# Moving a root chain to the end of a stage and reordering the last tiles of a hybrid DeltaNet and attention kernel

## Chip, cores and metric

The kernel runs on one core of a Trainium2 chip. A core has TensorE (PE, matrix products into the PSUM memory), VectorE (DVE), ScalarE (ACT), GpSimd (POOL) and SyncE (SP, which here issues most DMA transfers). The metric is the device time of one execution in microseconds; the median of three executions counts. All times in the text are microseconds, and those with a place ("at 354.0") are counted from the first instruction of the profiled execution.

## What is computed

Two layers over 512 latent tokens and 256 context tokens, 1024 wide, all in float32. Layer 0 is a bidirectional gated DeltaNet, layer 1 is grouped-query attention with a rotary embedding; each ends in a gated residual addition, and a last RMS norm gives the output.

```python
u = rms_norm(h, norm_g) * (1 + scale) + shift               # both layers
# layer 0
p = u @ w_in                                                # q: 8 heads, k: 8, v: 16, z: 16, of 128
qkv = silu(centred_dwconv(p[..., :DN_CONV_DIM], conv_w))    # 5 taps along the tokens
q = q * rsqrt(sum(q * q, -1) + 1e-6)                        # query norms; k likewise
o = forward and backward gated delta rule, in chunks of 64 tokens, context first, then latents
y = (rms_norm(o, o_norm_g) * silu(z)) @ w_out
# layer 1
y = (softmax(q k^T / sqrt(128)) v * silu(z)) @ w_out        # 8 query heads, 2 key heads
h = h + gate * y
return rms_norm(h_lat, final_norm_g)                        # (1, 512, 1024)
```

## The kernel before

Products that need float32 accuracy are made of three passes: each operand is split into a high and a low part, and high by high, high by low and low by high are summed in PSUM (the names wh and wl are the two parts of a weight, uh and ul those of the activations).

**The stage of the heads** lies between about 185 and 574 us. After the eight key heads, forty heads of the DeltaNet layer are worked in the order `zqzqzqqzqqzqqzvvzvvzvvzvvzvvzvvzvvzvvzzz`. Each is 48 matmuls for the 512 latent tokens and the 256 context tokens (L758, two PSUM banks out of four, so that a head takes the banks of the head two places before). A z head then needs a tanh on ACT (L781) and a gate step on DVE (L790), which reads the bank for the last time and so frees it. A v head needs a copy of the middle tap on ACT (L765), four taps on DVE (L773), a tanh on ACT (L783) and a step on DVE (L792), which frees the bank. Before each head its weights are loaded by SP (L739) and split by ACT (L744) and by DVE or POOL (L747). Beside the heads run other jobs: POOL solves triangular systems column by column (L643, L644, for three pairs of token tiles), multiplies the decays with the products of queries and keys (L545, into buffers named df, of which there are four, then stored by SP, L727), ACT computes the decays (L570, L572) from rows that SP loads (L557), and SP moves the results.

The sums of squares of the query heads come from PE (L810), and ACT copies them into `rq` (128 partitions by 6 tiles by 8 heads, 48 columns). The inverse root of `rq` is taken by `rsqrt_steps` (L185 to L204), eleven DVE instructions in a row that each read what the one before wrote. The text calls these the chain. The first later readers of `rq` are L1355 and L1088.

The order of all this on each engine is written by a planner in the kernel. Every job is a `Piece` with an engine, a cost, a due time, the pieces it comes after, the buffers it takes or holds, and an earliest time `since`. `ready_at` gives the time at which a piece could start on the planner's own clock (DVE pieces get a margin of 0.5), and `written_out` always writes next the piece that can start first, and among equals the one due first. On the chip every engine then works its list strictly in that order. The chain is one such piece of DVE (L1044), with a cost of 2.4 and a due time of `N * SLOT`, that is 40 x 8.8 = 352, and with no earliest time other than the end of the last copy into `rq`.

**The recurrence** follows (from about 574 us): its opening is the products of L1184 on PE, copies on ACT and the vd products on DVE (L1194). Then come the output projection of layer 0 (L1325) and the second layer.

**The last stage** begins at about 1151 us, where the attention's last gate step is done. For each of four tiles of 128 tokens, PE sums the output projection (L1845) into two PSUM banks of 512 columns. Per half, `finish_half` multiplies it by the gate (DVE, L1987), adds it to the residual `hs` (DVE, L1988) and squares and sums it on ACT (L1989). `finish_norm` turns the two sums into an inverse root by eight small DVE instructions (L1996 to L2000). Tiles 0 to 2 are scaled by that root and by the norm's weights `fg` in one DVE instruction (L2015) and sent by SP (L2006). For tile 3 each half is weighed by `fg` early (L2026); after the root, ACT scales the first half (L2028) and DVE the second (L2030), and ACT's and SP's queues send them. DVE works tile by tile: all of a tile's steps, then the next tile's. The row `jko` of two buffers holds the products of tiles 0 to 3 in turn.

Of the kernel before, what the change touches and what calls it, by code (L numbers as in the profile page):

```python
# [8 lines left out]
F32 = mybir.dt.float32  # L9
# [8 lines left out]
P = 128  # L18
D = 1024
# [67 lines left out]
def backbone(tc, a, out):  # L87
# [945 lines left out]
    for t, due in enumerate((170, 200, 230, 260, 290, 320)):  # L1033
# [5 lines left out]
        for v in range(2):  # L1039
# [4 lines left out]
    Piece("DVE", 2.4, N * SLOT, lambda: [f_() for f_ in rsqrt_steps(rq.rearrange("p t h -> p (t h)"), 1.0)], after=[last["rq", h] for h in range(QH)])  # L1044
# [857 lines left out]
    for u in range(32 + 4):  # L1902
# [82 lines left out]
    def finish_half(t, nh, jk):  # L1985
        c = slice(nh * 512, nh * 512 + 512)
        V.tensor_tensor(jk[:, c], acc[t][nh], gate1[:, 0, c], ALU.mult)  # L1987
        V.tensor_tensor(hs[t][:, c], hs[t][:, c], jk[:, c], ALU.add)  # L1988
        S.activation(jk[:, c], hs[t][:, c], AF.Square, accum_out=ss[:, t, nh:nh + 1])  # L1989
        if nh == 0:  # L1990
            V.tensor_scalar(ss[:, t, 0:1], ss[:, t, 0:1], 1.0 / D, EPS, ALU.mult, ALU.add)  # L1991

    def finish_norm(t):

        x, y, w = (f2.tile([P, 1], F32, tag=f"fr{i}", name=f"fr{i}_{t}") for i in range(3))
        V.tensor_scalar(x, ss[:, t, 1:2], 1.0 / D, ss[:, t, 0:1], ALU.mult, ALU.add)  # L1996
# [11 lines left out]
    for t in range(4):  # L2008
        jk = f2.tile([P, D], F32, tag="jko", name=f"jko{t}")
        if t < 3:  # L2010
            for k in range((KT, 6, 0)[t], KT):
                out_block(k, t, acc[t])
            for nh in range(2):
                finish_half(t, nh, jk)
            V.scalar_tensor_tensor(jk, hs[t], finish_norm(t), fg, ALU.mult, ALU.mult)  # L2015
            send(t, jk, slice(0, D), dma)
            if t == 0:
                load_hs(3)
        else:
            halves_ = [slice(0, 512), slice(512, D)]  # L2020
            hg = wp.tile([P, D], F32, tag="w", name="hg", bufs=3)
            for nh in range(2):
                for k in range(KT):
                    out_block(k, t, acc[t], (nh,))
                finish_half(t, nh, jk)
                V.tensor_tensor(hg[:, halves_[nh]], hs[t][:, halves_[nh]], fg[:, halves_[nh]], ALU.mult)  # L2026
            r = finish_norm(t)
            S.activation(hg[:, halves_[0]], hg[:, halves_[0]], AF.Copy, scale=r)  # L2028
            send(t, hg, halves_[0], nc.scalar.dma_start)
            V.tensor_scalar(hg[:, halves_[1]], hg[:, halves_[1]], r, None, ALU.mult)  # L2030
            send(t, hg, halves_[1], dma)
    written.__exit__(None, None, None)
    f2_c.__exit__(None, None, None)
    at_c.__exit__(None, None, None)
# [31 lines left out]
```

## Time and profile before

| | us |
|---|---|
| median of three executions (1184.9, 1194.69, 1189.23) | 1189.23 |
| the profiled execution | 1189.06 |
| its span, first to last instruction | 1187.2 |
| PE busy in the span | 1131.2 |
| mean granted clock of TensorE over the span | 0.987 |

In the rows of the order of time the columns are start, duration (both in us), engine, line, operation, output <- inputs, shapes, count, and in brackets the engine's idle time before it with what ended that. PEld is the loading of weights into PE, and runs beside it. In the table of stages the columns are the stretch, its length, then busy us and instructions of PE, PEld, DVE, ACT and POOL, then the granted clock of TensorE (1.00 is full), the busy share of the DMA engines and GB/s. In the list of waits the three numbers are total us, times and the longest. In the rows of one tile they are count, then shortest, median and longest duration in ns, and the first and last start.

### The profile page before, as it was taken

The page shows a single profiled execution, that of the slowest core. Times are in us where ns is not written, and L with a number is a line of the kernel's source. Part 1 is how long each engine was busy: PE and PEld are TensorE (multiplying, and loading weights), DVE is VectorE, ACT ScalarE, POOL GpSimd, SP SyncE. Part 2 cuts the span into 40 slices and gives each one's busy share as a digit, 9 for nine tenths or more (in the row PEclk, how much of TensorE's full clock was granted, in tenths as well). Part 3 has the DMA queues.
Part 4 walks back from the last instruction along what each step waited for, and adds up shares of the span by engine and source line. Part 5 has one row for each costly group of instructions (what it writes and reads, how often), then busy time and mean ns, then how long its engine had stood idle before and what let it go on. Part 6 is the DMA issues. An engine that isn't in the chain of part 4 may idle for free. (4 is left out here: it accounts for less than half of the span.)

```text
span 1187.2 us, 27636 instructions
## 1 busy us (share of the span) xinstructions
PE 1131.2 (95%) x10739; PEld 919.0 (77%) x10739; DVE 801.9 (68%) x1723; ACT 721.1 (61%) x1885; POOL 584.0 (49%) x443
## 2 busy tenths in 40 slices
PE   3998999999979999999999999899999999999995
PEld 1676778888868888888666666688887889999884
DVE  2669565889898777763588888546557466667646
ACT  3343333889666873874478998785753246666721
POOL 0130004499998998441285586555744244130900
PEclk9899999999999999999999999999999999999998
DMA  9477976866549544979599996475744112101323
GB/s 332 153 240 240 298 218 187 238 165 167 147 138 284 182 133 131 292 218 286 157 257 248 248 274 162 158 224 185 241 155 134 36 54 72 36 19 54 107 71 89
DMA packets 171124, 208.72 MB, mean 176 GB/s; under 512 B 12497, under 2 KB 126322, under 8 KB 170226
## 3 DMA queue, kind: packets, MB, share of 16 engines
q1 hardware_dynamic: 150914, 195.19, 55.7%
q10 hardware_dynamic: 20080, 11.77, 3.3%
q8 instruction: 85, 1.39, 0.5%
q14 instruction: 45, 0.37, 0.1%
HBM read 166.16 MB, written 40.67 MB: 174 GB/s over the span
## 5 line engine op out<-in xcount | busy, mean ns | idle before, releaser
L1325 PE MATMUL po<-woh,y 128*128 128x512 f32 x384 | 129.3, 401 | 0.7 <-ACT y L1301 0.7
L1167 POOL TENSOR_TENSOR S<-S,glb 128x512 f32<-128x512 f32 x80 | 81.7, 1042 | 70.0 <-PE ks L1158 70.0
L1274 POOL TENSOR_TENSOR wol<-wo,woh 128x1024 fp32r<-128x1024 f32 x32 | 77.1, 2412 | 54.6 <-ACT woh L1267 51.6
L644 POOL TENSOR_TENSOR X<-X,tmp 128x62 f32<-128x62 f32 (+15 forms) x93 | 97.0, 1043 | 7.3
L773 DVE SCALAR_TENSOR_TENSOR acc_v<-g_v,cwv,acc_v 128x510 f32<-128x510 f32 (+3 forms) x128 | 78.2, 615 | 31.9 <-ACT acc_v L765 28.2
L758 PE MATMUL g_v<-uh,wh_v 128*128 128x512 f32 (+1 forms) x256 | 89.4, 349 | 6.6 <-DVE sil_z L790 6.6
L643 POOL TENSOR_TENSOR tmp<-L,X 128x62 f32<-128x62 f32 (+15 forms) x93 | 86.4, 929 | 6.8
L758 PE MATMUL g_z<-uh,wh_z 128*128 128x512 f32 (+1 forms) x256 | 88.7, 346 | 0.0
L758 PE MATMUL g_v<-ul,wh_v 128*128 128x512 f32 (+1 forms) x256 | 87.2, 341 | 0.0
L758 PE MATMUL g_v<-uh,wl_v 128*128 128x512 f32 (+1 forms) x256 | 87.0, 340 | 0.0
L758 PE MATMUL g_z<-ul,wh_z 128*128 128x512 f32 (+1 forms) x256 | 86.6, 338 | 0.4 <-issue 0.4
L758 PE MATMUL g_z<-uh,wl_z 128*128 128x512 f32 (+1 forms) x256 | 86.7, 338 | 0.0
L1325 PEld LDWEIGHTS po<-woh,y 128*128 128x128 f32 x384 | 72.3, 188 | 15.9 <-ACT y L1301 0.9
L1325 PE MATMUL po<-wol,y 128*128 128x512 f32 x192 | 75.6, 394 | 0.9 <-POOL wol L1274 0.9
L333 POOL TENSOR_TENSOR wl_k<-w_k,wh_k 128x1024 fp32r<-128x1024 f32 x8 | 19.1, 2389 | 103.8 <-ACT wh_k L332 103.8
L758 PEld LDWEIGHTS g_v<-uh,wh_v 128*128 128x128 f32 x256 | 49.2, 192 | 12.4 <-DVE sil_z L790 6.9
L1299 DVE SCALAR_TENSOR_TENSOR pt<-pt,og,z 128x128 f32<-128x128 f32 x96 | 34.4, 358 | 34.3 <-PE pt L1290 31.5
L1232 DVE TENSOR_TENSOR S<-su,S 128x512 f32<-128x512 f32 x80 | 51.5, 686 | 6.0 <-PE su L1218 3.9
L1158 PE MATMUL ks<-S,ck 128*64 128x256 f32 x352 | 55.2, 392 | 0.4 <-ACT o L1164 0.4
L758 PEld LDWEIGHTS g_v<-uh,wl_v 128*128 128x128 f32 x256 | 49.2, 192 | 5.5
L758 PEld LDWEIGHTS g_z<-uh,wl_z 128*128 128x128 f32 x256 | 48.9, 191 | 5.7 <-issue 0.5
L758 PEld LDWEIGHTS g_z<-uh,wh_z 128*128 128x128 f32 x256 | 49.0, 192 | 5.3 <-issue 0.4
(432 smaller groups left out, 3342.5 us busy)
## 6 DMA issues: line engine op xcount, KB each, us to landing
aw<-in_ada_w SPq DMA_DIRECT2D x24, 1024.0 KB, 8.3
wo<-in_dn_w_out SPq DMA_DIRECT2D x32, 512.0 KB, 3.4
cv<-v_d SPq DMA_DIRECT2D x48, 256.0 KB, 7.8
w_z<-in_dn_w_in SPq DMA_DIRECT2D x16, 512.0 KB, 5.0
w_v<-in_dn_w_in SPq DMA_DIRECT2D x16, 512.0 KB, 4.6
v_d<-vt ACTq DMA_DIRECT2D x16, 384.0 KB, 4.1
cT<-t_d SPq DMA_DIRECT2D x12, 512.0 KB, 8.3
ckt<-kt_d SPq DMA_DIRECT2D x12, 512.0 KB, 6.6
```

The costliest lines, as they stand in the source:

```text
L333: E.tensor_tensor(wl[:, :, :m], w[:, :, :m], wh[:, :, :m], ALU.subtract)
L643: G.tensor_tensor(tv, bcast(L[:, :, j + 1:, j], 3, j + 1), bcast(X[:, :, j, 0:j + 1], 2, n), ALU.mult)
L644: G.tensor_tensor(X[:, :, j + 1:, 0:j + 1], X[:, :, j + 1:, 0:j + 1], tv, ALU.subtract)
L758: T.matmul(ps[:, :m], w[:, k], u[:, k, c0:c0 + m], start=k == 0 and n_ == 0, stop=k == KT - 1 and n_ == 2)
L773: V.scalar_tensor_tensor(acc[:, c0 + lo:c0 + hi], ps[:, lo + j - 2:hi + j - 2], cwv[:, j, ct:ct + 1], acc[:, c0 + lo:c0 + hi], ALU.mult, A ...
L1158: T.matmul(ks[r0:r0 + 64, w], kq[w][:, hh, r0:r0 + 64], St[hh][:, d], start=True, stop=True)
L1167: G.tensor_tensor(St[hh], St[hh], bcast(g_, 3, P), ALU.mult)
L1232: V.tensor_tensor(St[hh], sj, St[hh], ALU.add)
L1274: G.tensor_tensor(wl, raws.pop(n), halves[n][0], ALU.subtract)
L1299: V.scalar_tensor_tensor(pj, pj, og, raw(z, off, [[st_, 2], [1, 64]]), ALU.mult, ALU.mult)
L1325: T.matmul(acc[:, nh], y[i][:, j, :], ww[k][:, nh * 512:(nh + 1) * 512], start=h == 0 and x == 0, stop=h == VH - 1 and x == 2)
```

## The change

Two places. First, the chain gets an earliest time of 376.0 on the planner's clock and a due time 5 units sooner:

```diff
-    Piece("DVE", 2.4, N * SLOT, lambda: [f_() for f_ in rsqrt_steps(rq..., 1.0)], after=[last["rq", h] for h in range(QH)])
+    Piece("DVE", 2.4, N * SLOT - 5, lambda: [f_() for f_ in rsqrt_steps(rq..., 1.0)], after=[last["rq", h] for h in range(QH)], since=376.0)
```

Second, the last stage is written anew. PE works a tile's 512-column pieces one after the other rather than both per step of the sum, and tile 3's second half as two pieces of 256 columns. DVE's order is interleaved: while the sums of one tile are with ACT, DVE works products of the next. The sums are folded in one by one (`finish_sum`). Tiles 0 and 1 have the two buffers of `jko`, tile 2 gets a buffer of its own (the room of an attention buffer that is no longer used), and tile 3 takes tile 0's.

```diff
-                ss = f2.tile([P, 4, 2], F32, tag="ss", name="ss", bufs=1)
+                ss = f2.tile([P, 4, 3], F32, tag="ss", name="ss", bufs=1)
...
+    jks = [f2.tile([P, D], F32, tag="jko", name=f"jko{t}") for t in range(2)]
+    CHUNKS = [((0, 512), (512, 512))] * 3 + [((0, 512), (512, 256), (768, 256))]
...
+    def finish_part(t, i):
+        c0, n = CHUNKS[t][i]
+        c, (bank, b0) = slice(c0, c0 + n), divmod(c0, 512)
+        jk = jks[t]
+        V.tensor_tensor(jk[:, c], acc[t][bank][:, b0:b0 + n], gate1[:, 0, c], ALU.mult)
+        V.tensor_tensor(hs[t][:, c], hs[t][:, c], jk[:, c], ALU.add)
+        S.activation(jk[:, c], hs[t][:, c], AF.Square, accum_out=ss[:, t, i:i + 1])
+
+    def finish_sum(t, i):
+        if i == 0:
             V.tensor_scalar(ss[:, t, 0:1], ss[:, t, 0:1], 1.0 / D, EPS, ALU.mult, ALU.add)
+        else:
+            V.tensor_scalar(ss[:, t, 0:1], ss[:, t, i:i + 1], 1.0 / D, ss[:, t, 0:1], ALU.mult, ALU.add)
...
+    out_tile(2)
+    finish_part(0, 0)
+    finish_part(0, 1)
+    finish_sum(0, 0)
+    finish_part(1, 0)
+    r = finish_row(0)
+    finish_part(1, 1)
+    out_tile(3)
+    finish_sent(0, r)
+    load_hs(3)
+    finish_sum(1, 0)
+    r = finish_row(1)
+    finish_sent(1, r)
+    jks.append(at.tile([P, NT, 256], F32, tag="pT0", name="jko2").rearrange("p t c -> p (t c)")[:, 0:D])
+    jks.append(f2.tile([P, D], F32, tag="jko", name="jko3"))
...
+    finish_part(2, 0)
+    finish_part(2, 1)
+    finish_sum(2, 0)
+    r = finish_row(2)
+    finish_part(3, 0)
+    finish_sent(2, r)
+    weighed(0)
+    finish_sum(3, 0)
+    finish_part(3, 1)
+    weighed(1)
+    finish_sum(3, 1)
+    finish_part(3, 2)
+    weighed(2)
+    finish_sum(3, 2)
+    r = finish_norm(3)
```

`finish_row` is the second `finish_sum` and `finish_norm`; `finish_sent` scales a tile by the root and `fg` and sends it; `weighed` multiplies a piece of tile 3 by `fg`. The scaling and sending of tile 3 behind its root is unchanged.

More of the change, by code (lines that the diff above doesn't have):

```diff
@@ L1043, in backbone @@
             kept(("QK", t, v), Piece("SP", 0.4, due + 14, q_store, t, v, after=[pr], holds=[("df", r[v])], lands=4.0))
-    Piece("DVE", 2.4, N * SLOT, lambda: [f_() for f_ in rsqrt_steps(rq.rearrange("p t h -> p (t h)"), 1.0)], after=[last["rq", h] for h in range(QH)])
+    Piece("DVE", 2.4, N * SLOT - 5, lambda: [f_() for f_ in rsqrt_steps(rq.rearrange("p t h -> p (t h)"), 1.0)], after=[last["rq", h] for h in range(QH)], since=376.0)
     x = N * SLOT - 60
@@ L1983, in backbone, with out_chunk @@
     acc = [pg, acc1, [tr_tile(f"pso2{nh}").rearrange("p a b -> p (a b)") for nh in range(2)], [s_all[:, 1024:1536], po]]
[L1985 to L1987 removed]
+    jks = [f2.tile([P, D], F32, tag="jko", name=f"jko{t}") for t in range(2)]
+    CHUNKS = [((0, 512), (512, 512))] * 3 + [((0, 512), (512, 256), (768, 256))]
+    def out_chunk(k, t, c0, n):
+        cc_, (bank, b0) = slice(c0, c0 + n), divmod(c0, 512)
+        for x, (i, j) in enumerate(PASS):
+            T.matmul(acc[t][bank][:, b0:b0 + n], yT[i][:, k, t * P:(t + 1) * P], wo[j][:, k, cc_], start=k == 0 and x == 0, stop=k == KT - 1 and x == 2)
+    def finish_part(t, i):
[3 more added lines that the diff above has]
+        V.tensor_tensor(jk[:, c], acc[t][bank][:, b0:b0 + n], gate1[:, 0, c], ALU.mult)
         V.tensor_tensor(hs[t][:, c], hs[t][:, c], jk[:, c], ALU.add)
[L1989 to L1990 removed]
+        S.activation(jk[:, c], hs[t][:, c], AF.Square, accum_out=ss[:, t, i:i + 1])
+    def finish_sum(t, i):
+        if i == 0:
             V.tensor_scalar(ss[:, t, 0:1], ss[:, t, 0:1], 1.0 / D, EPS, ALU.mult, ALU.add)
+        else:
+            V.tensor_scalar(ss[:, t, 0:1], ss[:, t, i:i + 1], 1.0 / D, ss[:, t, 0:1], ALU.mult, ALU.add)
     def finish_norm(t):
[L1995 to L1996 removed]
+        x = ss[:, t, 0:1]
+        y, w = (f2.tile([P, 1], F32, tag=f"fr{i}", name=f"fr{i}_{t}") for i in range(2))
         V.tensor_scalar(y.bitcast(I32), x.bitcast(I32), -0.5, float(0x5F3759DF - 0x400000), ALU.mult, ALU.add)
@@ L2006, in send @@
             q(out[0, c_ * 64:c_ * 64 + 64, c], x[hf * 64:hf * 64 + 64, c])
[L2008 to L2031, printed above, removed]
@@ new lines, in finish_row, with finish_sent, out_tile @@
+    def finish_row(t):
+        finish_sum(t, 1)
+        r = finish_norm(t)
+        return r
+    def finish_sent(t, r):
+        V.scalar_tensor_tensor(jks[t], hs[t], r, fg, ALU.mult, ALU.mult)
+        send(t, jks[t], slice(0, D), dma)
+    for k in (6, 7):
+        out_block(k, 1, acc[1])
+    def out_tile(t):
+        for c0, n in CHUNKS[t]:
+            for k in range(KT):
+                out_chunk(k, t, c0, n)
+    out_tile(2)
+    finish_part(0, 0)
+    finish_part(0, 1)
+    finish_sum(0, 0)
@@ new lines, in backbone, with weighed @@
+    finish_part(1, 0)
[9 more added lines that the diff above has]
+    jks.append(f2.tile([P, D], F32, tag="jko", name="jko3"))
+    hg = wp.tile([P, D], F32, tag="w", name="hg", bufs=3)
+    def weighed(i):
+        c0, n = CHUNKS[3][i]
+        V.tensor_tensor(hg[:, c0:c0 + n], hs[3][:, c0:c0 + n], fg[:, c0:c0 + n], ALU.mult)
@@ new lines, in backbone @@
+    finish_part(2, 0)
[13 more added lines that the diff above has]
+    r = finish_norm(3)
+    S.activation(hg[:, 0:512], hg[:, 0:512], AF.Copy, scale=r)
+    send(3, hg, slice(0, 512), nc.scalar.dma_start)
+    V.tensor_scalar(hg[:, 512:], hg[:, 512:], r, None, ALU.mult)
@@ L2032, in backbone @@
+    send(3, hg, slice(512, D), dma)
     written.__exit__(None, None, None)
```

## The prediction

> **What bounds the kernel now.** I read the page's busy times first, then the table of stages, then who waited for whom, then the order of time around the two places that the change touches.
>
> ```profile
> PE 1131.2 (95%) x10739; PEld 919.0 (77%) x10739; DVE 801.9 (68%) x1723; ACT 721.1 (61%) x1885; POOL 584.0 (49%) x443
> ```
>
> TensorE (PE) is busy 95% of the span, so time is won only where PE stands still or crawls, or behind its last matmul. The waits of PE between 185 and 600 us and the stages around the worst of them:
>
> ```profile
> PE g_v L758 <- DVE sil_z L790: 6.6, 1, 6.6
> ```
> ```profile
> 348.00:355.00 7.00, 0.37 (x2) 0.27 (x2) 6.86 (x8) 1.65 (x3) 6.76 (x6) 0.67 0.38 131
> 355.00:361.00 6.00, 6.00 (x16) 4.67 (x16) 5.85 (x8) 0.60 (x1) 5.69 (x5) 0.53 0.74 240
> ```
>
> From 348 to 355 PE does nothing (0.37 us busy) while VectorE (DVE) is busy 6.86 of 7 us, and in the next 6 us PE is busy throughout but at a granted clock of 0.53. The order of time shows what DVE did there:
>
> ```profile
> 338.39 1.48 DVE L747 TENSOR_TENSOR wl_v<-w_v,wh_v 128x1024 fp32r<-128x1024 f32 x1 [0.34 <-ACT wh_v L744]
> 339.79 1.21 DVE L194 TENSOR_SCALAR rq<-rq 128x48 f32<-128x48 f32 x1
> ...
> 352.94 1.15 DVE L202 SCALAR_TENSOR_TENSOR rq<-rs,rs 128x48 f32<-128x48 f32 x1
> 354.00 1.00 DVE L790 SCALAR_TENSOR_TENSOR sil_z<-sil_z,g_z 128x512 f32<-128x512 f32 x2
> ```
> ```profile
> 340.69 0.60 ACT L781 ACTIVATE sil_z<-g_z 128x512 f32<-128x512 f32 x1
> ```
> ```profile
> 342.26 1.19 POOL L644 TENSOR_TENSOR X<-X,tmp 128x494 f32<-128x494 f32 x1
> ...
> 359.08 2.04 POOL L644 TENSOR_TENSOR X<-X,tmp 128x504 f32<-128x504 f32 x1
> 365.22 4.77 POOL L545 TENSOR_TENSOR df_1q<-df_1q,KQ 128x1024 f32<-128x1024 f32 x2 [4.11 <-DVE KQ L721]
> ```
> ```profile
> 347.28 0.82 PE L379 MATMUL tr_v<-ident,sil_v 128*128 128x128 f32 x6
> 354.73 0.79 PE L758 MATMUL g_v<-uh,wh_v 128*128 128x512 f32 x1 [6.63 <-DVE sil_z L790]
> ...
> 360.77 0.39 PE L758 MATMUL g_v<-uh,wl_v 128*128 128x512 f32 x1
> 361.00 0.40 PE L758 MATMUL g_v<-uh,wh_v 128*128 128x512 f32 x1
> ```
>
> The root chain of the query norms is eleven instructions on 48 columns; the planner costs it at 2.4 us, and it held DVE from 339.79 to 354.00, 14.2 us. Behind it stood head 16's gate step L790, whose tanh was done at 340.69 + 0.60 = 341.3. That step frees the PSUM bank in which head 18's product has to start, so PE, out of work at 348.1, waited 6.63 us and then came back slow.
>
> **Part one, the chain moved to the end of the heads.** What it removes: with the chain gone, L790 runs at 341.3, its bank is free at about 342, and PE goes on at 348.1: 6.63 us. The slow return goes with it: from 354.73 to 360.77 fourteen matmuls take 6.04 us; at the later spacing of 0.23 us (360.77 to 361.00) they take 3.22 us, so 2.8 us. Ceiling for this place: 6.63 + 2.8 = 9.4 us. [...]
>
> How much of it lasts depends on what is not tied to PE. GpSimd (POOL) solves a triangular system in a row of updates and is late by its own work; the only time it stood still from 342 to 466 is the 4.11 us before 365.22, for KQ, which comes from PE and DVE and is early after the change. So POOL gains at most 4.1 us. I take off one collision: L644 takes 1.19 us at 342.26 but 2.04 at 359.08, beside large DVE work, and DVE's large work of 361 to 365 now meets a busy POOL; 0.9 us, so POOL gains 3.2 to 4.1. What hangs on POOL later:
>
> ```profile
> 482.19 1.54 ACT L570 ACTIVATE df_4q<-df_4q,gcV 128x64 f32<-128x64 f32 x6 [2.20 <-DMA df_4q<-gc_d]
> ```
> ```profile
> 492.57 0.98 DVE L792 SCALAR_TENSOR_TENSOR sil_v<-g_v,acc_v 128x512 f32<-128x512 f32 x2
> ```
> ```profile
> 495.63 0.50 PE L758 MATMUL g_v<-uh,wh_v 128*128 128x512 f32 x1
> ```
>
> The load of df_4q needs a buffer that POOL's q_prod (L545) and its store free. ScalarE (ACT) waits for it already (2.20 us), and behind it in ACT's order stand head 30's steps, which lead to the L792 at 492.57 (done after some 0.7 us, 493.3), which frees the bank for head 32 at 495.63. PE's margin there is 2.4 us. So PE can keep POOL's 3.2 to 4.1 us plus 2.4, which is 5.6 to 6.5; I take **6.0**, with 3.2 (no margin left) and 9.4 (POOL never binds) as ends. From there to the end of the heads PE has no wait in the trace, and the later loads are issued on PE's, DVE's or ACT's signal, so the gain passes through.
>
> What it adds: the same eleven instructions, no DMA, on DVE where the planner's clock passes 376.5 (since 376.0 and a margin of 0.5). Working its list of before through with its own costs, for the order only, the chain stands at 174.3 of that clock, ahead of head 16's gate, as the trace has it; its spot closes within 4 units, so the rest of the order stays. Head 37's gate steps stand at 374.9 and 376.5, head 38's at 387.0. The chain thus falls beside the second step of head 37:
>
> ```profile
> 555.38 0.69 DVE L790 SCALAR_TENSOR_TENSOR sil_z<-sil_z,g_z 128x512 f32<-128x512 f32 x1 [4.36 <-ACT sil_z L781]
> 556.94 0.42 DVE L790 SCALAR_TENSOR_TENSOR sil_z<-sil_z,g_z 128x256 f32<-128x256 f32 x1 [0.87 <-ACT sil_z L781]
> 567.29 1.02 DVE L790 SCALAR_TENSOR_TENSOR sil_z<-sil_z,g_z 128x512 f32<-128x512 f32 x2 [9.93 <-ACT sil_z L781]
> ...
> 576.53 0.20 DVE L1355 TENSOR_TENSOR or<-rq 128x48 f32<-128x48 f32 x1
> ```
> ```profile
> 581.53 2.04 POOL L1167 TENSOR_TENSOR S<-S,glb 128x512 f32<-128x512 f32 x2 [30.11 <-PE ks L1158]
> ```
>
> DVE idles 9.93 us there, POOL 30.11 us. With POOL silent the nearest row for one instruction on 48 columns is L1355's 0.20 us: 11 x 0.2 = 2.2 us, hidden in the 9.93; even the old 14.2 would overrun the hole by little. Queued behind it on DVE is at most the L790 of 556.94, and for that the store of head 37's gate on SP's queue, with the loads behind it of matrices used past 579 us. Its reader L1355 comes 18 us later. Cost taken: zero; without the cover, 2.2.
>
> **Part two, the last stage.** Rows of the tail, PE, then DVE:
>
> ```profile
> 1163.86 5.76 PE L1845 MATMUL s<-wo,yT 128*128 128x512 f32 x24
> 1169.46 5.76 PE L1845 MATMUL po<-wo,yT 128*128 128x512 f32 x24
> ```
> ```profile
> 1151.27 0.68 DVE L1987 TENSOR_TENSOR jko<-pg,gate 128x512 f32<-128x512 f32 x1
> ...
> 1171.49 0.21 DVE L1996 TENSOR_SCALAR fr<-ss 128x1 f32<-128x1 f32 x1 [0.79 <-ACT jko L1989]
> 1173.60 1.29 DVE L2015 SCALAR_TENSOR_TENSOR jko<-hs,fr,fg 128x1024 f32<-128x1024 f32 x1
> 1174.80 0.68 DVE L1987 TENSOR_TENSOR jko<-s,gate 128x512 f32<-128x512 f32 x1
> 1177.72 0.68 DVE L1987 TENSOR_TENSOR jko<-po,gate 128x512 f32<-128x512 f32 x1
> 1182.03 0.49 DVE L2030 TENSOR_SCALAR hg<-hg,fr 128x512 f32<-128x512 f32 x1
> ```
>
> PE's last product ends at 1175.22, but DVE, still busy with tile 2 and the first half of tile 3, takes it up at 1177.72: 2.5 us late. From there to the scale r (ready at 1182.03) are 4.31 us. The change orders DVE's work so that the waits for ACT's sums (0.79 us) mostly fall behind other work, and makes the last piece 256 columns wide:
>
> ```profile
> 564.42 0.28 PE L758 MATMUL g_z<-ul,wh_z 128*128 128x256 f32 x1
> 564.54 0.28 PE L758 MATMUL g_z<-uh,wl_z 128*128 128x256 f32 x1
> ```
> ```profile
> 1150.06 0.43 DVE L1837 SCALAR_TENSOR_TENSOR po<-po,zt 128x256 f32<-128x256 f32 x1 [6.41 <-PE po L1831]
> 1150.53 0.37 ACT L1839 CAST yT<-po 128x256 fp32r<-128x256 f32 x1 [7.33 <-DVE po L1837]
> 1150.93 0.42 DVE L1840 TENSOR_TENSOR yT<-po,yT 128x256 fp32r<-128x256 f32 x1 [0.44 <-ACT yT L1839]
> ```
> ```profile
> L1988 DVE TENSOR_TENSOR hs<-hs,jko x8: 691/692/694, 1152.0 to 1178.4; 128x512 f32<-128x512 f32 x8
> L1989 ACT ACTIVATE jko<-hs x8: 629/632/632, 1152.8 to 1179.2; 128x512 f32<-128x512 f32 x8
> ```
>
> PE: 48 matmuls at the spacing of 0.12 instead of 24 in 5.60 us (1163.86 to 1169.46): 5.76, so PE ends 0.2 us later, at 1175.4. DVE's load ahead of the last piece, from 1151.27: six products and sums of tiles 0 to 2 at 0.68 + 0.69 + gaps, 1.44 each, 8.6; three norms at 2.11 (1171.49 to 1173.60), 6.3; five small sums at no more than 0.21, 0.8; three scalings at 1.2, 3.6; tile 3's first 512 and 256 columns, 1.44 + 0.85; their weighings by fg, 1.1; one wait for ACT, 0.8. Together 23.5: free at 1174.8, so PE sets the end. The last chain is 4.31 less (0.68 - 0.43) + (0.69 - 0.42) + (0.63 - 0.37) = 3.53, from 1175.4 to 1178.95 instead of 1182.03: 3.1 us. The count of DVE's load is good to half a microsecond, so I take **2.7**, between 2.2 and 3.1. What follows r (two products, four sends) is the same. The moved loads and sends on SP: tile 3's residual is loaded behind tile 0's send, a microsecond or so later than now, and read at about 1171; the third tile's own buffer frees it from tile 0's send. Both free.
>
> **Sum.** 6.0 + 2.7 = 8.7 us off the profiled execution's 1189.06 (span 1187.2 and 1.9 around it; the median of the runs, 1189.23, is the same within 0.2): **1180.4 us**, -0.7%.
>
> **Rivals.** *POOL never binds.* The whole 9.4 us stays: 9.4 + 2.7 = 12.1, 1177.0 us. For it: POOL's load may run smoother; against it: ACT's 2.20 us wait. 0.2. *The pause comes back.* If PE stops again about head 32 for what POOL can't give, and returns slow, the 2.8 us go once more: 3.2 + 2.7 = 5.9, 1183.2 us. 0.13. *The list doesn't do what it says.* If emptying the spot reshuffles the order into another stall like it, only the tail is won: 1186.4. 0.06. *Slower.* The chain falls behind the last gate step, where DVE's vd products open the recurrence (from 575 us), and costs 14.2 us there as before: 14.2 - 8.7 = +5.5, 1194.6. It decides from 8.7 / 11 = 0.8 us an instruction. Against it: head 38's steps stand 10 units behind it, and POOL rests. 0.04. [...]
>
> **Numbers.** The forecast has 0.57. Its own range is 1179 to 1184 (5.4 to 9.6 us). Eight in ten: 1175 (the 12.4 us of both ceilings, and the runs' spread) to 1187 (tail alone). A measurement of this kernel tells about 1% from no change; 1% is 1177.2 us, which only the first rival reaches, about half the time, and the forecast sometimes: faster 0.18; slower by 1% needs more than the last rival: 0.04; within 0.78.
>
> **What would show it.** Right: no PE wait for sil_z L790 near 350 us and a clock near 1.00 there; rq's chain near 550 us at about 0.2 us an instruction; POOL's 4.11 us wait gone; PE waiting near head 32 or not; the last L1987 starting right at PE's end, and r 3 to 4 us behind it. Wrong: a new PE pause between 360 and 570 us, a chain of 1 us instructions at the heads' end, or DVE still behind PE at the last piece.

## The result and the profile after

| | runs | median (lowest to highest), us | ratio to before, 95% interval |
|---|---|---|---|
| before | 22 | 1191.07 (1183.92 to 1195.76) | |
| after | 22 | 1185.92 (1178.04 to 1193.88) | 0.9957 (0.9938 to 0.9977) |

The change wins 5.1 us (2.7 to 7.4), where 8.7 had been forecast. The profiled execution of the changed kernel took 1193.14 us, span 1191.4, so it can't be compared end to end: its first head starts at 176.93 us where the one of before starts at 171.59 (169.4 to 173.9 in the twelve other profiles of this study), before anything that the change touches. Stages are therefore compared by their own lengths.

The table of stages for the changed kernel, the same two stretches as before (columns as told there):

```profile
348.00:355.00 7.00, 7.00 (x168) 6.32 (x168) 5.22 (x6) 5.34 (x9) 6.76 (x6) 1.00 0.20 59
355.00:361.00 6.00, 6.00 (x56) 4.89 (x56) 5.03 (x10) 2.08 (x5) 5.92 (x3) 1.00 0.98 336
```

PE no longer stops, and its granted clock is 1.00 where it was 0.53. The order of time of DVE at the chain's new place:

```profile
556.78 0.69 DVE L790 SCALAR_TENSOR_TENSOR sil_z<-sil_z,g_z 128x512 f32<-128x512 f32 x1 [4.35 <-ACT sil_z L781]
557.38 0.18 DVE L194 TENSOR_SCALAR rq<-rq 128x48 f32<-128x48 f32 x1
...
559.76 0.21 DVE L202 SCALAR_TENSOR_TENSOR rq<-rs,rs 128x48 f32<-128x48 f32 x1
559.89 0.41 DVE L790 SCALAR_TENSOR_TENSOR sil_z<-sil_z,g_z 128x256 f32<-128x256 f32 x1
```

The same eleven instructions take 2.6 us (557.38 to 559.97) instead of 14.2, between the two gate steps of head 37, in a hole. So far this is the forecast. But the list of PE's waits between 185 and 600 us has a new first line:

```profile
PE g_z L758 <- DVE sil_v L792: 3.5, 2, 2.7
```

The shorter of the two, 0.77 us, stands before head 22. The longest is here, in the order of time of PE, then of DVE, then of POOL:

```profile
484.90 0.50 PE L758 MATMUL g_z<-uh,wh_z 128*128 128x512 f32 x1 [2.69 <-DVE sil_v L792]
...
485.93 0.60 PE L758 MATMUL g_z<-ul,wh_z 128*128 128x512 f32 x1
...
488.89 0.61 PE L758 MATMUL g_z<-uh,wl_z 128*128 128x512 f32 x1
489.31 0.42 PE L758 MATMUL g_z<-uh,wh_z 128*128 128x512 f32 x1
```
```profile
469.64 3.41 DVE L648 TENSOR_TENSOR X<-X,bball 128x1024 f32<-128x1024 f32 x1 [5.18 <-POOL X L644]
472.97 3.42 DVE L747 TENSOR_TENSOR wl_z<-w_z,wh_z 128x1024 fp32r<-128x1024 f32 x1
476.31 1.21 DVE L648 TENSOR_TENSOR X<-X,bball 128x1024 f32<-128x1024 f32 x1
...
484.16 0.68 DVE L792 SCALAR_TENSOR_TENSOR sil_v<-g_v,acc_v 128x512 f32<-128x512 f32 x1
```
```profile
469.56 5.74 POOL L545 TENSOR_TENSOR df_2q<-df_2q,KQ 128x1024 f32<-128x1024 f32 x2
471.91 3.39 POOL L545 TENSOR_TENSOR df_2q<-df_2q,KQ 128x1024 f32<-128x1024 f32 x1
```

(The second row is the later one of the pair, shown alone.) To be read from the bottom: POOL's solve ends at 469.56, DVE has waited 5.18 us for it and starts L648 at 469.64, in the same moment as POOL starts two products of its own. Both crawl: DVE's L648 and L747 take 3.41 and 3.42 where the L648 at 476.31 takes 1.21, and POOL's pair takes 5.74, where the pair at 487.10 takes 4.75. The rows show them taking turns: POOL's first product ends at 471.96, after its usual 2.40 us, L648 ends 1.1 us behind it, POOL's second 2.3 us behind that, and L747 1.1 us behind that. So the two engines' work comes almost one after the other (6.8 us in all, 2.4 and 4.75 alone), and DVE is 4.4 us late. Behind that stand the taps and the gate step L792 for which PE waits 2.69 us before head 31; from 485.93 to 489.31, a microsecond after PE has gone on, eight matmuls come at 0.42 us instead of 0.23, which is half clock (granted 0.50 from 485.94 to 489.36).

The end of the program, PE and then DVE:

```profile
1169.40 5.76 PE L1991 MATMUL s<-wo,yT 128*128 128x512 f32 x24
1175.00 5.83 PE L1991 MATMUL po<-wo,yT 128*128 128x256 f32 x48
```
```profile
1178.33 0.15 DVE L2003 TENSOR_SCALAR ss<-ss 128x1 f32<-128x1 f32 x1
1180.86 0.42 DVE L1997 TENSOR_TENSOR jko<-po,gate 128x256 f32<-128x256 f32 x1 [2.39 <-PE po L1991]
...
1182.45 0.41 DVE L1997 TENSOR_TENSOR jko<-po,gate 128x256 f32<-128x256 f32 x1
...
1186.01 0.49 DVE L2076 TENSOR_SCALAR hg<-hg,fr 128x512 f32<-128x512 f32 x1
```

DVE is no longer behind PE: it idles 2.39 us. But the product at 1180.86 is the first of the two 256-column pieces, whose 24 matmuls were done some 3 us earlier. It waits for PE's very last matmul (1175.00 + 5.83 = 1180.83), and both pieces are then worked one after the other. The root is ready 5.19 us behind PE's end instead of 6.81.

The lengths of the stages, each the difference between the starts of the first rows of its ends in the order of time ("heads" from head 14 to the first L1184, "recurrence" from there to the first L1325; last column from PE's last matmul to the root's use), in us. Kernels below the second line are told of in the next section.

| | head 17 to 19 | head 30 to 32 | heads | recurrence | PE's end to root |
|---|---|---|---|---|---|
| before | 29.69 | 19.88 | 264.18 | 175.57 | 6.81 |
| after | 20.05 | 24.46 | 259.84 | 180.15 | 5.19 |
| before_again | 28.99 | 19.89 | 263.86 | 175.56 | 6.81 |
| before_third | 29.39 | 19.88 | 263.08 | 178.46 | 6.81 |
| after_again | 20.04 | 23.61 | 257.52 | 175.63 | 5.19 |
| chain_only | 20.05 | 21.84 | 263.63 | 176.73 | 6.81 |
| tail_only | 28.92 | 19.88 | 262.06 | 175.56 | 5.19 |
| third_bank | 20.05 | 22.23 | 258.51 | 176.72 | 3.61 |
| early_psum | 23.15 | 23.14 | 260.82 | 179.98 | 6.82 |
| relief | 20.05 | 22.10 | 260.10 | 178.32 | 5.19 |
| spread | 20.05 | 21.89 | 256.08 | 177.03 | 5.19 |
| best | 20.04 | 22.06 | 259.72 | 177.27 | 3.61 |
| best2 | 20.05 | 21.48 | 255.37 | 179.94 | 3.61 |
| spread_before | 28.51 | 19.88 | 262.77 | 176.11 | 6.81 |

So the changed kernel wins 9.64 us from head 17 to head 19, loses 2.84 + 1.74 of it between heads 30 and 32 and 0.7 in all elsewhere, and keeps 4.3 at the end of the heads.

### The profile page after: what moved, and what is told of

Its sections match the earlier page's. It is cut to its first block, busy times and chain, and to the rows that moved or that the text cites. A ratio compares the mean times of both kernels' runs of the same rounds, so it can differ in the third digit from the quotient of the medians.

```text
span 1191.4 us, 27692 instructions
## 1 busy us (share of the span) xinstructions
PE 1138.2 (96%) x10763; PEld 925.1 (78%) x10763; DVE 793.3 (67%) x1727; ACT 721.4 (61%) x1887; POOL 585.7 (49%) x443
## 5 line engine op out<-in xcount | busy, mean ns | idle before, releaser
L1325 PE MATMUL po<-woh,y 128*128 128x512 f32 x384 | 129.3, 401 | 0.7 <-ACT y L1301 0.7
L1325 PEld LDWEIGHTS po<-woh,y 128*128 128x128 f32 x384 | 72.3, 188 | 15.9 <-ACT y L1301 0.9
L1325 PE MATMUL po<-wol,y 128*128 128x512 f32 x192 | 75.5, 393 | 0.9 <-POOL wol L1274 0.9
L758 PEld LDWEIGHTS g_z<-ul,wh_z 128*128 128x128 f32 x256 | 49.4, 193 | 5.0 <-issue 0.2
L1158 PE MATMUL ks<-S,cq 128*64 128x256 f32 x352 | 52.9, 379 | 0.0
```

What stands on the lines that cost most here:

```text
L758: T.matmul(ps[:, :m], w[:, k], u[:, k, c0:c0 + m], start=k == 0 and n_ == 0, stop=k == KT - 1 and n_ == 2)
L1158: T.matmul(ks[r0:r0 + 64, w], kq[w][:, hh, r0:r0 + 64], St[hh][:, d], start=True, stop=True)
L1325: T.matmul(acc[:, nh], y[i][:, j, :], ww[k][:, nh * 512:(nh + 1) * 512], start=h == 0 and x == 0, stop=h == VH - 1 and x == 2)
```

## The experiments

### The two parts alone, and the end with a bank of its own

In the edits `...` stands for code left out.

**Chain alone.** The kernel before with the first of the two changes and no other, so with the last stage as before:

```diff
-    Piece("DVE", 2.4, N * SLOT, lambda: ..., after=...)
+    Piece("DVE", 2.4, N * SLOT - 5, lambda: ..., after=..., since=376.0)
```

> Only the chain is moved; the last stage is that of before. Theory: the 9.4 us pause at head 18 goes (the span from the start of head 17 to that of head 19 falls from 29.7 to about 20 us), PE stops for some 2.7 us before head 31 because DVE waits for POOL's solve, and from head 14 to the start of the recurrence some 4.3 us are left. On this theory the 4.4 us that the profiled execution of the changed kernel lost again in the recurrence are DMA landings of that execution, so the recurrence takes 175.6 us here as before and the median is about 4 us below before. Rival: an earlier start of the recurrence itself makes it 4 to 5 us longer (180.2 us as in the changed kernel), and the median is within 1 us of before.

Measured: 1186.13 us (1178.68 to 1194.57, 12 runs) against 1191.70 (28 runs), ratio 0.9955 (0.9931 to 0.9979). Its profile has the 9.64 us at head 19, and then loses nearly all: 3.8 us in three waits for L792 (2.15 before head 22, 0.38 before head 31, where 2.7 had been expected, and 1.24 before head 32), 3.1 us in one wait of PE at a short product (L671, 0.8 before) that the list of waits charges to no engine, and some at half clock (0.76 granted on average from 385 to 392 us). The part pays, but by how much differs from one execution to the next.

**Last stage alone.** The changed kernel with the chain at its old place:

```diff
-    Piece("DVE", 2.4, N * SLOT - 5, lambda: ..., after=..., since=376.0)
+    Piece("DVE", 2.4, N * SLOT, lambda: ..., after=...)
```

> Only the last stage is changed; the chain stays at its old place. Theory: the tail gains 1.8 us, not the 2.7 of the prediction, because the first 256 columns of tile 3's second half are taken up only when the last matmul of both pieces is done, so the two pieces run one after the other behind PE (1.6 us from the first L1997 product to the second). From the start of the last 512 columns on PE to the root 11.0 us, against 12.6 before. The median is about 1.8 us below before. Rival (the prediction): 2.7 us, with only the last 256 columns behind PE.

Measured: 1187.74 us (1185.06 to 1192.57, 12 runs), ratio 0.9969 (0.9952 to 0.9986), 3.7 us (1.7 to 5.7). Its profile has the root 5.19 us behind PE's end, as in the changed kernel: from the start of tile 2's sums to the root 27.82 us instead of 29.37, so 1.55 us, and not the 1.8 expected. That gain is the same in every execution: from PE's first product `s<-wo,yT` (at 1136.82 before) to the root it takes 45.2 us in all six profiles with the old last stage and 43.65 in all five with the new one. The runs show somewhat more; what the rest is, the profile doesn't tell.

**A bank for the last piece.** The changed kernel with tile 3's last 256 columns summed in another PSUM bank:

```diff
+    def sums(t, c0, n):
+        bank, b0 = divmod(c0, 512)
+        return pg[0][:, 0:n] if t == 3 and b0 else acc[t][bank][:, b0:b0 + n]
...
-            T.matmul(acc[t][bank][:, b0:b0 + n], ...)
+            T.matmul(sums(t, c0, n), ...)
...
-        V.tensor_tensor(jk[:, c], acc[t][bank][:, b0:b0 + n], gate1[:, 0, c], ALU.mult)
+        V.tensor_tensor(jk[:, c], sums(t, c0, n), gate1[:, 0, c], ALU.mult)
```

> The changed kernel with the last 256 columns summed in a bank of their own (tile 0's first, free by then). Theory that the two pieces are tied because they share one bank's buffer: the first piece's product starts about 2.9 us before PE's end and the root comes 1.6 us earlier than in the changed kernel, 3.5 us after PE's last matmul rather than 5.2. Rival, that DVE is simply late: the root stays 5.2 us behind PE's end. The heads behave as in the changed kernel; a second look at the recurrence's length with the chain moved.

Measured: 1184.57 us (1178.71 to 1191.67, 9 runs), ratio 0.9945 (0.9918 to 0.9972). The order of time of its end, PE and DVE:

```profile
1166.35 2.99 PE L1995 MATMUL po<-wo,yT 128*128 128x256 f32 x24
1169.18 3.00 PE L1995 MATMUL pg<-wo,yT 128*128 128x256 f32 x24
```
```profile
1169.75 0.41 DVE L2001 TENSOR_TENSOR jko<-po,gate 128x256 f32<-128x256 f32 x1
...
1172.22 0.42 DVE L2001 TENSOR_TENSOR jko<-pg,gate 128x256 f32<-128x256 f32 x1 [0.81 <-PE pg L1995]
...
1175.79 0.49 DVE L2080 TENSOR_SCALAR hg<-hg,fr 128x512 f32<-128x512 f32 x1
```

Now DVE works the first piece at 1169.75, while PE sums the last, and the root stands 3.61 us behind PE's end (1172.18): 1.58 us sooner than in the changed kernel. What tied the two pieces together was the place that they shared: DVE takes the first piece up at PE's end, 1180.86, with one bank, and 2.4 us ahead of PE's end, at 1169.75, with two. The bank is also one tile of the program, and this run gives the last piece another bank and another tile at once, so which of the two ties them is not shown; the row of after has DVE wait for PE's last matmul into that tile.

### Why the chain took 14 us

> The kernel before, with the root chain at its old early place, but its running estimate y held in a PSUM tile, so that no instruction of the chain reads two operands from SBUF. Theory: the 14.2 us of the chain before are one mechanism, DVE instructions with two SBUF operands that end only as an instruction of POOL ends (in the trace of before the chain's instructions end at 341.00, 342.25, 343.51, 344.69, 345.97 and POOL's at 340.96, 342.18, 343.45, 344.63, 345.90, while L195, with one operand, takes 0.19 us in their midst). Then the chain takes 3 to 5 us here, most of the 6.63 us wait of PE and its slow return are gone, and head 17 to head 19 takes 20 to 22 us rather than 29.7; the time comes out near the one with the chain alone moved, 3 to 6 us under before. Rival: every small DVE instruction beside POOL is slow whatever it reads; then the chain stays at 10 to 14 us and head 17 to 19 at 26 to 30 us.

The edit, in the kernel before (the chain is still written early, but the planner puts it one gate step later, and from there on it also orders DVE's, ACT's and SP's lists anew, so the length of the chain can be compared and the time of the whole only roughly):

```diff
-    Piece("DVE", 2.4, N * SLOT, lambda: [f_() for f_ in rsqrt_steps(rq..., 1.0)], after=...)
+    def chain_in_psum():
+        x = rq.rearrange("p t h -> p (t h)")
+        y = pa.tile([P, 512], F32, tag="tr", name="rq_room")[:, 0:NT * QH]
...
+    Piece("DVE", 2.4, N * SLOT, chain_in_psum, after=..., takes=["tr"], lands=0.1)
```

The middle of the chain in the kernel before, DVE and POOL:

```profile
341.04 0.19 DVE L195 TENSOR_SCALAR rs<-rq 128x48 int32<-128x48 int32 x1
341.27 0.98 DVE L200 SCALAR_TENSOR_TENSOR rs<-rq,rs 128x48 f32<-128x48 f32 x1
342.28 1.23 DVE L201 TENSOR_TENSOR rs<-rs,rs 128x48 f32<-128x48 f32 x1
343.55 1.14 DVE L202 SCALAR_TENSOR_TENSOR rs<-rs,rs 128x48 f32<-128x48 f32 x1
```
```profile
341.04 1.14 POOL L643 TENSOR_TENSOR tmp<-L,X 128x494 f32<-128x494 f32 x1
```

and the same steps in early_psum:

```profile
345.39 0.21 DVE L1049 TENSOR_SCALAR rq_room<-rq 128x48 int32<-128x48 int32 x1
345.64 0.21 DVE L1051 SCALAR_TENSOR_TENSOR rq_t<-rq_room,rq 128x48 f32<-128x48 f32 x1
345.88 0.20 DVE L1052 TENSOR_TENSOR rq_t<-rq_t,rq_room 128x48 f32<-128x48 f32 x1
...
347.58 0.20 DVE L1053 SCALAR_TENSOR_TENSOR rq<-rq_t,rq_room 128x48 f32<-128x48 f32 x1
```
```profile
345.39 1.19 POOL L644 TENSOR_TENSOR X<-X,tmp 128x494 f32<-128x494 f32 x1
346.66 1.11 POOL L643 TENSOR_TENSOR tmp<-L,X 128x504 f32<-128x504 f32 x1
```

With one operand in PSUM the chain takes 2.8 us (344.96 to 347.78) beside a busy POOL. Before, the nine instructions with two SBUF operands each last until an instruction of POOL ends (341.04 + 1.14 = 342.18, and DVE's ends at 342.25; the other eight too end 0.06 to 0.07 us behind one of POOL), and L195, with a single operand, takes 0.19. So ten of the chain's eleven rows fit the theory that two SBUF operands make the difference. The first doesn't fit so simply: L194 has one input, and yet took 1.21 us before (339.79 to 341.00) and 0.40 in early_psum, each time ending with an instruction of POOL; no run shows why. So the cost was neither the chain's length nor its place alone, but its meeting with POOL. The time, 1186.98 us (1184.19 to 1193.90, 9 runs) against 1191.44 (22 runs), ratio 0.9957 (0.9934 to 0.9979), is that of the chain moved; head 17 to 19 takes 23.15 us, somewhat over the expected 20 to 22, and what the new order of the lists has to do with that isn't shown.

### Where the gain goes near head 31

**Two products off POOL.** Of the changed kernel:

```diff
-            G_ = v == 0 or t not in ()
+            G_ = v == 0 or t not in (0, 1)
```

> The changed kernel, with two of the twelve products of decays with KQ (the second direction's, for token tiles 0 and 1, L545) on DVE instead of POOL. Theory: after the change POOL sets the pace of the second half of the heads. In the changed kernel's trace its solve ends at 469.6 and DVE's L648, waiting 5.18 us for it, starts there; PE then waits 2.69 us before head 31 and comes back at half clock, some 7 us lost in all. Two products of 2.4 to 3.4 us each leave POOL, so L648 should start 4.8 to 6.8 us sooner counted from head 14, PE's wait before head 31 should be gone, and head 14 to the first recurrence product (259.8 in the changed kernel's profile, 264.2 before) should come to 253 to 256; the time should fall by 3 to 6 us below the changed kernel's. Rival one: PE's wait before head 31 hangs on the loads of the decay rows (the df_4q load that ACT waits 1.87 us for), not on POOL; then head 14 to the recurrence stays at 258 to 260. Rival two: what POOL is spared, DVE pays: the two products on DVE run into POOL's updates and delay DVE's gate steps near 355 and 371, and PE stops there instead, 1 to 3 us.

Measured: 1187.28 us (1182.71 to 1196.49, 10 runs), ratio 0.9971 (0.9947 to 0.9994): no better than the change. POOL did get ahead: counted from head 14, the two L648 start 2.2 and 5.5 us sooner. But the heads take 260.10 us. The planner, which knows of the moved cost, had rewritten the order, and around the solve's end it reads, DVE and POOL:

```profile
462.10 6.74 DVE L648 TENSOR_TENSOR X<-X,bball 128x1024 f32<-128x1024 f32 x2 [8.01 <-POOL X L644]
468.75 0.67 DVE L790 SCALAR_TENSOR_TENSOR sil_z<-sil_z,g_z 128x512 f32<-128x512 f32 x1
```
```profile
462.02 5.73 POOL L545 TENSOR_TENSOR df_2q<-df_2q,KQ 128x1024 f32<-128x1024 f32 x2
```

Two L648 in a row take 6.74 us (2 x 1.21 alone) beside POOL's pair, and this time a gate step that PE waits for stands behind them. Neither the theory (POOL's pace alone) nor the rivals as written fit: what costs is that DVE's and POOL's large work start in the same moment, whenever the solve ends. The same two products off POOL, together with the bank for the last piece (best):

> The changed kernel with both mends: tile 3's last 256 columns summed in a PSUM bank of their own (so that DVE can take the first 256 while PE works the last), and two products of decays on DVE instead of POOL. If the theory of POOL's pace holds, the gains add: 1.6 us at the end as with the bank alone (root 3.6 us behind PE's end) and 3 to 6 us in the heads, 1179 to 1182 as a median, against some 1191 before. If the wait before head 31 hangs on something else, it stays at the 1184.6 of the bank alone, within the spread of the runs.

Measured: 1183.84 us (1180.42 to 1186.58, 6 runs), ratio 0.9935 (0.9911 to 0.9959), within the spread of the bank alone.

**The meeting taken away.** The changed kernel with the two products of token tile 2 issued on DVE, at the same places of the written order; PE, ACT and SP keep their lists:

```diff
-            pr = Piece(..., 2.5 if G_ else 1.5, due + 8, q_prod, t, v, G if G_ else V, after=[ma, d_[v]], ...)
+            pr = Piece(..., 2.5 if G_ else 1.5, due + 8, q_prod, t, v, V if t == 2 else G if G_ else V, after=[ma, d_[v]], ...)
```

> The changed kernel with only this: the two products of decays and KQ for token tile 2 (L545, df_2q) are issued on DVE instead of POOL, at the same places of the written order, so that nothing else moves on any engine. In the changed kernel's trace POOL starts them at 469.56, the moment its solve ends, and DVE starts L648 at 469.64: POOL's two take 5.74 (4.75 without company), DVE's L648 and L747 3.41 and 3.42 (1.21 without), so DVE is 4.4 us late at its next steps, and PE then waits 2.69 us before head 31 for the L792 at 484.16 and comes back at half clock. Theory: that meeting of DVE and POOL, which the kernel before had as well but behind PE's old delay, is what gives the gain back. Without it DVE works the first product in the 5.2 us in which it waits for POOL's solve, and the second at 1.2 us after L747; L662 should start some 3 us sooner (about 158.8 after head 14, 162.1 in the changed kernel), PE's wait before head 31 should be under 0.6 us, head 30 to head 32 should take 20 to 21 us (24.5 and 23.6 in two profiles of the changed kernel), and head 14 to the recurrence 254 to 256 (259.8 and 257.5). The time should be 2 to 5 us under the changed kernel's. Rival: the load of df_4q that ACT waits 1.87 us for sets the pace there; then the wait only moves to head 32 and head 14 to the recurrence gains less than 1.5 us.

Measured: 1182.89 us (1176.54 to 1187.72, 7 runs) against 1193.31 (12 runs), ratio 0.9913 (0.9880 to 0.9946). DVE around the solve's end, then PE:

```profile
456.67 1.22 DVE L545 TENSOR_TENSOR df_2q<-df_2q,KQ 128x1024 f32<-128x1024 f32 x1
463.56 1.23 DVE L648 TENSOR_TENSOR X<-X,bball 128x1024 f32<-128x1024 f32 x1 [5.67 <-POOL X L644]
464.70 1.22 DVE L747 TENSOR_TENSOR wl_z<-w_z,wh_z 128x1024 fp32r<-128x1024 f32 x1
465.84 1.22 DVE L545 TENSOR_TENSOR df_2q<-df_2q,KQ 128x1024 f32<-128x1024 f32 x1
466.97 1.22 DVE L648 TENSOR_TENSOR X<-X,bball 128x1024 f32<-128x1024 f32 x1
```
```profile
475.66 0.50 PE L758 MATMUL g_z<-uh,wh_z 128*128 128x512 f32 x1 [1.16 <-DVE sil_v L792]
476.00 0.40 PE L758 MATMUL g_z<-ul,wh_z 128*128 128x512 f32 x1
```

Every large DVE instruction is back at 1.22 us, although DVE now does two more; POOL's pair is gone, and PE's wait falls from 2.69 to 1.16 us without half clock behind it (0.23 us a matmul). That is more than the expected 0.6; L662 starts 2.3 us sooner, not 3, and head 30 to 32 takes 21.89, not 20 to 21. The heads take 256.08 us, just above what was expected, 3.8 and 1.4 less than in the two profiles of the changed kernel. One wait says little, since with the old list it was 0.38 (chain_only) to 3.20 us (after_again). Two other figures say more. From the end of POOL's solve to L662 it takes 4.6 us instead of 7.8, although the solve itself ends no sooner (155.3 us behind head 14, 154.3 in after), so it is DVE that got faster, and not POOL. And PE's waits for gate steps from head 14 on come to 3.2 to 4.1 us in the four profiles with the old list (after, after_again, chain_only, third_bank), but to 1.7 here and 1.5 in best2 below. The rest of the wait still hangs on the end of the solve.

**The same in the kernel before:**

> The kernel before, with the chain at its early place, and only the two products of tile 2 (L545, df_2q) issued on DVE instead of POOL. Theory: the meeting of POOL and DVE at the end of POOL's solve is there in the kernel before too, but hidden, because PE is 9 us later after its pause at the chain; so taking it away alone is worth nothing: head 30 to head 32 stays at 19.9 us, head 14 to the recurrence within 1.5 us of 264.2 and 263.9, and the time is that of the kernel before within 1 us. Rival: the products on DVE are a gain of their own, 2 to 5 us, whatever the chain does. For the recurrence (175.6 us in three profiles of kernels with PE's pause at the chain, 175.6 to 180.2 in nine without it): if the longer ones belong to the earlier arrival, it is 175.6 here; if they fall on any execution, it can be longer here too.

Measured: 1191.03 us (1188.16 to 1197.92, 10 runs) against 1191.09 (13 runs), ratio 1.0002 (0.9969 to 1.0035). Heads 30 to 32 take 19.88 us as in every kernel with the old pause. The meeting was there before, hidden behind PE's own lateness; it costs only once the chain is gone.

**Bank and products together:**

> The kernel with a PSUM bank of its own for tile 3's last 256 columns, and with the two products of tile 2 on DVE as in the run before. If the two gains add, 1180 to 1183 as a median where the kernel before has 1191: 1.6 us from the bank at the end, 2 to 5 from the products. If the products only move the wait, it stays at the 1184.6 of the bank alone.

Measured: 1179.08 us (1177.03 to 1181.06, 6 runs) against 1193.31 (12 runs), ratio 0.9879 (0.9851 to 0.9907), 14.4 us (11.1 to 17.8). The changed kernel's interval, 0.9938 to 0.9977, lies wholly above: this version is faster than both kernels. So does that of the bank alone, 0.9918 to 0.9972, and with it the runs too show a gain from the two products; between spread and the changed kernel alone the intervals still overlap.

### What belongs to the execution

The kernel before, the changed kernel and the kernel before once more, all unaltered:

> The kernel before, a second profile. If the spread of the executions lies in the start and in DMA landings: the start of head 4 moves by some microseconds against 215.7, while the stretch from head 14 to the recurrence stays at 264.2 us within 0.5. The length of the recurrence (175.6 us) shows how much of it changes from one execution to the next.

> The changed kernel once more, unaltered, for a second profile. Theory: the recurrence (first L1184 to first L1325) is 1.2 to 4.6 us longer whenever the chain is at the end of the heads (180.15, 176.73 and 176.72 in three profiles of such kernels, 175.56 or 175.57 in three of kernels that have it early), so it is 176.5 or more here. Rival: the difference is one of executions; then it can be 175.6 here. The start-up (to head 0), 176.98 in the changed kernel's first profile and 170.3 to 171.8 in the five others, should be back at 170 to 172. From head 17 to head 19 20.05 us in any case.

> The kernel before once more, unaltered, for a third profile. If the recurrence (first L1184 to first L1325) is longer only where PE comes early, it is 175.6 as in the two others, without a wait of PE at L1210. If its length is a matter of the execution, a wait of 0.7 to 3.2 us there is possible here too. Head 17 to head 19 should be 29 to 29.7 us.

One execution each: 1187.76, 1179.92 and 1191.99 us. The recurrence, 4.6 us longer in the first profile of the changed kernel than before, is 175.63 in its second, and 178.46 in the third profile of the kernel before. The order of time of PE, the changed kernel and then before_third:

```profile
610.59 0.44 PE L1210 MATMUL pq<-vn,cQK 64*64 64x128 f32 x6 [2.09 <-issue]
```
```profile
607.48 0.44 PE L1210 MATMUL pq<-vn,cQK 64*64 64x128 f32 x6 [1.81 <-issue]
```

PE waits there in some executions for nothing that the profile shows ("issue"), in kernels of both kinds. The five profiles with the old pause have 175.56 to 178.46, the nine without it 175.63 to 180.15; whether coming early makes such waits likelier stays open, and so does their cause. One lead is in the traces: where such a wait is over 1.4 us, the loads of `cv` issued 10 to 15 us ahead of it took 9 to 13 us to land (12.1 to 13.0 in after); in the other executions the same loads took 7 to 10 (7.3 to 8.5 in before). The half clock behind head 31 also differs between executions. Here is after_again at that place:

```profile
477.57 0.50 PE L758 MATMUL g_z<-uh,wh_z 128*128 128x512 f32 x1 [3.20 <-DVE sil_v L792]
477.91 0.40 PE L758 MATMUL g_z<-ul,wh_z 128*128 128x512 f32 x1
478.15 0.40 PE L758 MATMUL g_z<-uh,wl_z 128*128 128x512 f32 x1
```

A longer wait, 3.20 us, and PE goes on at 0.24 us a matmul: full clock. The traces show a difference. In those of before and after, the granted clock changes only on a grid of 3.41 us (to half at 350.40 and back at 360.64, three steps later, in the one; at 485.94 and 489.36 in the other), whose place is another in each of the two. Here are steps of that length around head 31, first of the changed kernel and then of after_again (columns as in the table of stages):

```profile
482.53:485.94 3.41, 1.04 (x5) 0.87 (x6) 3.30 (x7) 1.54 (x6) 0.00 (x0) 1.00 0.72 192
485.94:489.36 3.42, 3.42 (x10) 2.68 (x9) 3.35 (x9) 3.42 (x14) 2.26 (x1) 0.50 0.89 301
```
```profile
472.47:475.88 3.41, 1.90 (x16) 1.69 (x15) 3.27 (x6) 0.60 (x1) 0.00 (x0) 1.00 1.00 320
475.88:479.30 3.42, 1.73 (x7) 1.42 (x8) 3.35 (x7) 2.30 (x8) 0.00 (x0) 1.00 0.75 199
479.30:482.71 3.41, 3.41 (x16) 2.82 (x15) 3.30 (x8) 3.38 (x12) 2.93 (x2) 1.00 1.01 336
```

The wait of 2.69 us fell into one step, in which PE was busy only 1.04 us, and the next step had half clock; the wait of 3.20 us was split between two steps with 1.90 and 1.73 us busy, and the clock stayed full. From head 14 to the recurrence, half clock followed a step at full clock with PE busy 1.11 us in before and 1.26 in chain_only, and no other step at full clock there in before and after had PE busy for less than 2.08. It is a reading of the traces that no run tested, and at the program's start it fails: in before a step with 2.49 us busy (26.13 to 29.55) was followed by half clock.

## Why the prediction was partly wrong

**Right.** The ceiling of part one (9.4 forecast; 9.64 measured, 8.9 and 9.3 against the two other profiles of before), the chain's new place and its cost (2.2 forecast, 2.6 measured, hidden), and the unchanged order of the rest (on DVE only the chain moves, on SP one store). That POOL's lateness would take gain back near heads 31 and 32, with a slow return of PE (at half clock), was foreseen as a rival.

**POOL's gain.** Forecast 3.2 to 4.1, as the wait of 4.11 us less one collision of 0.9. The wait is gone, but POOL's solve ends only 2.7 us sooner (156.9 us behind head 14 before, 154.2 after): its pairs L545 near 352 and 369 take 5.75 and 5.71 instead of 4.70 and 4.77, so the collisions that took the place of the wait were under-counted.

**The path, the margin, and the pause that comes back.** The prediction led POOL's pace to PE by the load of df_4q, ACT and the L792 before head 32, with a margin of 2.4 us. In the changed kernel PE stops one head earlier, before head 31, and by another path: the solve, then DVE's L648 and L747 beside POOL's pair, then L792. The margin before head 31 (from the end of the gate step that frees its bank to its first matmul) was 3.56 us in the profile that the prediction had, and 2.7 + 3.56 is the 6.3 us that PE did keep up to there (head 31 starts 169.57 us behind head 14, 175.88 before). So the sum was built rightly, but with the margin of one execution: in before_again, before_third and tail_only, which have the same list of the heads, it is 2.94, 2.01 and 1.25 us before head 31, and 2.05, 0.44 and 0.16 before head 32 in place of the 2.4. And it took a wait there to cost its own length only: in the first profile PE came back at half clock and 4.3 us were left, in the second it did not and 6.7 were. The four profiles with this order of the heads keep 0.6 to 6.7 of the 264.18 us, 4.3 on average; the four of the old order average 263.3, and against that it is 3.4. So the step of part one that failed is its term of 6.0: POOL's gain was counted too high, the margin was that of one execution, and the half clock of the return was left out. The 6.0 was one outcome among several, and a good one, taken as the typical; the rival that had the pause in its sum, with a chance of 0.13, came nearest (5.9 us).

**Part two.** Forecast 2.7 from 2.2 to 3.1, measured 1.55. The load of DVE was counted right (it was idle at PE's end). The step that failed is the last chain of 3.53 us: it assumed that the first 256 columns were worked while PE summed the last. Both lie in one bank and tile, and DVE got them only at PE's end (1180.86). With two the chain measured 3.61, and the part 3.1 us.

**The gain passes through the recurrence.** In the first profile it seemed not to; three profiles of before and two of after show that this length differs between executions by as much as 4.6 us, in the kernel before by 2.9.

In sum: 5.1 us measured against 8.7. By the profiles the heads gave 3.4 of the 6.0 and the last stage 1.55 of the 2.7, together 5.0; that this meets the runs within 0.1 us is luck, with four profiles on a side. What the meeting of DVE and POOL holds back in the heads is shown by spread and spread_before, 1.4 to 3.8 us by the profiles of spread and the changed kernel; the runs' intervals are too wide to size it better.

## What to carry to other kernels

Taking away a stall is worth its length only up to the next engine's margin, so ask which two engines will now start large work in the same moment, and stagger those first: here the change won 5 us, and 10 (6 to 14) with two products moved (spread). Where a late piece is cut in two so that one half can be worked while the other is summed, give each half a PSUM bank and a tile of its own; here the root then stood 3.61 us behind PE's end instead of 5.19 (third_bank). And look at two or three profiles of each kernel before reading a margin or explaining a few microseconds; here a margin read as 2.4 us was 0.2 to 2.4 in four profiles, and a stage far from the change differed by 4.6 us between executions.

## What the runs showed of the hardware

- The chain's nine DVE instructions on 48 columns with both inputs in SBUF took 0.21 us each with POOL idle (after) and 0.98 to 2.32 beside POOL (before); with one input in PSUM the rows of early_psum have 0.20 to 0.21 beside the same POOL work.
- Two large instructions of DVE and two of POOL that met ran almost one after the other (after, from 469.56): DVE's L648 and L747 took 3.41 and 3.42 us instead of 1.21 each, POOL's pair 5.74 instead of 4.75, 6.8 us in all.
- A wait of PE of 2.69 us was followed by 3.4 us at half clock (after, 485.94 to 489.36), one of 3.20 us in another execution by none (after_again), and the one of 6.63 us before the change by 6.0 us. In the first two it went with how the wait fell on steps of 3.41 us: PE busy 1.04 us in a step, then half clock; 1.90 and 1.73, then full.
